# Four doubles of each up projection by Strassen's scheme, in a two-layer decoder trunk

## The chip, the cores and the metric

The kernel runs on one core of one Trainium2 chip. The metric is the device time of one execution in microseconds, median of three runs. Engines are called as the profile calls them: PE is TensorE (PEld its weight loads), DVE VectorE, ACT ScalarE, POOL GpSimd, SP SyncE. A number with an L is a line of the kernel's source.

## The reference

x is one sequence of 512 tokens by 1024 features, all in float32. Layer 0 is a Mamba-2 mixer, then a ConvFFN. Layer 1 is differential attention, then a ConvFFN with weights of its own. The change touches the two ConvFFNs alone:

```python
FFN_DIM = 2816
def conv_ffn(x, ln_g, up_w, conv_w, conv_b, down_w):
    u = causal_dwconv(rms_norm(x, ln_g) @ up_w, conv_w, conv_b)   # width 3 along the tokens
    gate, up = u[..., :FFN_DIM], u[..., FFN_DIM:]
    return (jax.nn.silu(gate) * up) @ down_w
def rms_norm(x, g):
    y = x * lax.rsqrt(jnp.mean(x * x, axis=-1, keepdims=True) + EPS)
    return y * g
...
    x = x + conv_ffn(x, ffn_ln_g[layer], ffn_up_w[layer], ...)
```

## The kernel before

Every product is made three times: an operand is split into a high part (rounded to fp32r by ACT) and a low part (the rest, by DVE), and a product is high x high + high x low + low x high. `mm3` (L207 to L210) issues the three.

The stream x lies transposed in SBUF: features on the partitions, 512 tokens along the free axis, as eight blocks `xT[k]`. For an FFN, `scaled` writes x times the norm's gain into `xgh[k]` and `xgl[k]`. The norm's factor of each token isn't in them; it is a row `rr[0]` (the tile `nr_f`), made from sums over features while the first pair of products runs.

The 2816 features of gate and up are handled as 22 pairs: pair p is 128 columns of gate and the same of up. `products` takes a weight chunk of 1024 x 128 for each and issues 24 matmuls of 512 columns into one PSUM bank. `taps` multiplies the bank by `rr[0]` into `u` (L1021), applies the bias and the last tap on ACT (L1022) and two taps on DVE (L1024). Then follow Silu of gate (L1272), the multiplication (L1276) and `operands`.

The down projection is already done by Strassen's scheme: two pairs (an even and an odd p) by two halves of tokens give a 2 x 2 matrix of operands, and seven products in the order `SEVEN[l]`, named 1 to 7, take the place of eight. `operands` forms the seven operand sides `sh`, `sl` from an even and an odd pair: some are the halves themselves, the others sums of them. Products 5 and 1 in Layer 0, and product 1 in Layer 1, read sides made of the even pair alone. Weights are summed in memory too: `combine` starts accumulating DMAs on POOL's queue.

The pairs come in three parts, `PARTS_D`: pairs 0 to 5, 6 to 13, 14 to 21. After a part's pairs comes its down projection, `down_features` in Layer 0 (matmuls of 256 columns, added to x by L1217) or `down_tokens` in Layer 1 (matmuls of 512 columns, added to `xr` by L1150). In Layer 1 x is first transposed into `xr` (`residual`, L1037).

Weights run through one list, `plan`, in the order in which the products use them. `chunk` hands out the next chunk and first emits those up to two further on: a load on SP's queue, a high split on ACT (L148 or L1079), a low split on DVE (L159 or L1080). There are three raw, three high and three low buffers. A scheduler lays out each engine's instructions before the run, by their place in the program and by when their inputs are ready. In the FFNs PE's order comes from it as well. While Layer 0's FFN runs, `key_weights_in` and `key_weights_out` also scale the key weights for Layer 1 and write them back to memory.

Of the kernel before, what the change touches and what calls it, by code (L numbers as in the profile page):

```python
# [31 lines left out]
PARTS_D = (0, 6), (6, 14), (14, 22)  # L32
# [10 lines left out]
def trunk_kernel(ctx: ExitStack, tc, x, ssm_ln_g, ssm_in_w, ssm_conv_w, ssm_conv_b, ssm_dt_bias,  # L43
# [47 lines left out]

    def ffn_plan(l):
        for p0, p1 in PARTS_D:
            for p in range(p0, p1):
                plan.append(("g%d_%d" % (l, p), *w_cols(ffn_up_w[l], 0, KB, p * P, P)))
                plan.append(("u%d_%d" % (l, p), *w_cols(ffn_up_w[l], 0, KB, FFN + p * P, P)))
            nq = (p1 - p0) // 2
            for m in SEVEN[l]:
                for c in range(0, nq, 2) if l else range(2):
                    plan.append(("s%d%s_%d_%d" % (l, m, p0, c), (l, m, p0, c, min(2, nq - c) if l else nq)))  # L100
# [24 lines left out]
    state = {"next": 0, "use": 0}  # L125
# [3 lines left out]
    class Weights:  # L129


        def __init__(self, i, behind=None):
# [7 lines left out]
            sync.dma_start(self.cols(self.raw), src)  # L140
# [48 lines left out]
    def emit_chunk():  # L189
        i = state["next"]  # L190
        if i < len(plan):
            state["next"] = i + 1
            if len(plan[i]) == 2:
                state["combine"](plan[i][0], *plan[i][1][1:])
                return
            with tc.issue_after(state["rs"]) if i < 5 else nullcontext():
                Weights(i).split()
# [329 lines left out]
    def run(gen):  # L527
        for _ in gen:
            pass
# [435 lines left out]
    def key_weights_in(pl, n, behind):  # L965
        t = pl.tile([P, 1024], F32, tag="stage", name="stage%d" % n, bufs=1)
# [14 lines left out]
    def bias_ranges(pl, behind):  # L981
        rb = pl.tile([AH, 32], F32, name="rb")
# [4 lines left out]
        for i in range(2):  # L987
            bv = pl.tile([AH, hb], F32, name="bv%d" % i)
# [9 lines left out]
    def ffn(l, norm, bp, gnext, nnext):  # L998
        with tc.tile_pool(name="ffn_h%d" % l, bufs=1) as hp, tc.tile_pool(name="ffn%d" % l, bufs=1) as fp:
            rr = []  # L1000

            def products(j, p, c=None):
                key = "%s%d_%d" % ("gu"[j], l, p)
                wh, wl = chunk(key)
                ps = mm_bank("ps_" + key)
                for k in range(KB):
                    last = mm3(ps, wh[:, k, :], wl[:, k, :], xgh[k], xgl[k], k == 0, k == KB - 1)
                    if c is not None and k == KB - 2:
                        with tc.issue_after(last):
                            rr.append(norm.row(c))  # L1010
                return ps

            def taps(j, p, ps):
                key = "%s%d_%d" % ("gu"[j], l, p)
                r = rr[0]
                col = lambda t: cf[l][:, 88 * j + 22 * t + p:88 * j + 22 * t + p + 1]
                u = fp.tile([P, T], F32, tag="u", name="u" + key, bufs=3)
                v = fp.tile([P, T], F32, tag="v%d" % j, name="v" + key, bufs=3 if j else 4)
                if nnext is None and key in ("g1_1", "u1_1"):
                    residual(j)  # L1020
                dve.tensor_tensor(out=u, in0=ps, in1=r, op=ALU.mult)  # L1021
                act.activation(v, u, AF.Identity, bias=col(3), scale=col(2))  # L1022
                for s in range(1, 3):
                    dve.scalar_tensor_tensor(out=v[:, s:], in0=u[:, :T - s], scalar=col(2 - s),  # L1024
                                             in1=v[:, s:], op0=ALU.mult, op1=ALU.add)
                return v

# [26 lines left out]
            def ahead(p0, n, behind):  # L1054

                for k, j, i in (("z", 0, 0), ("x", 0, 1), ("y", 1, 1)) if l else (("x", 0, 0), ("z", 0, 1)):
                    for c in range(0, n // 2, 2) if l else range(2):
                        nq = min(2, n // 2 - c) if l else n // 2
# [677 lines left out]
```

## Time and profile before

| | |
|---|---|
| median of three runs | 1314.41 us (1313.95 to 1314.45) |
| the profiled execution | 1314.37 us, span 1312.7 us |
| busy | PE 1307.3 us, DVE 1073.9, ACT 713.9, POOL 177.1 |
| granted TensorE clock | 1.000 |
| moved by DMA | 167.84 MB, 128 GB/s on average |
| Layer 0's FFN | from 376.6 us to about 728 us of the span |
| Layer 1's FFN | from about 960 us to the end |

A row of a group gives line, engine, operation, names and shapes, count, then busy time and mean duration, then the engine's idle time before these instructions and what ended it. A row in order of time gives start, duration, engine, line, operation. A row by stage gives the stretch, then each engine's busy time and count, the granted clock, and the share and rate of DMA. Matmuls overlap in the trace, so their pace is the distance between starts, not the duration.

### The profile page before, as it was taken

The page shows a single profiled execution, that of the slowest core. Times are in us where ns is not written, and L with a number is a line of the kernel's source. Part 1 is how long each engine was busy: PE and PEld are TensorE (multiplying, and loading weights), DVE is VectorE, ACT ScalarE, POOL GpSimd, SP SyncE. Part 2 cuts the span into 40 slices and gives each one's busy share as a digit, 9 for nine tenths or more (in the row PEclk, how much of TensorE's full clock was granted, in tenths as well). Part 3 has the DMA queues.
Part 4 walks back from the last instruction along what each step waited for, and adds up shares of the span by engine and source line. Part 5 has one row for each costly group of instructions (what it writes and reads, how often), then busy time and mean ns, then how long its engine had stood idle before and what let it go on. Part 6 is the DMA issues. An engine that isn't in the chain of part 4 may idle for free.

```text
span 1312.7 us, 18264 instructions
## 1 busy us (share of the span) xinstructions
PE 1307.3 (100%) x6771; PEld 1096.3 (84%) x6771; DVE 1073.9 (82%) x1774; ACT 713.9 (54%) x1156; POOL 177.1 (13%) x244
## 2 busy tenths in 40 slices
PE   9999999999999999999999999999999999999998
PEld 8878888888888998898889887777888888888887
DVE  7889878888888877876888878678778878887886
ACT  6696554743344545543556667777654544544452
POOL 5330200300021401020113210000020100010001
PEclk9999999999999999999999999999999999999999
DMA  7543533432234656774767763222225446453635
GB/s 210 161 152 87 151 99 108 140 96 82 88 91 137 126 144 200 177 163 121 206 174 150 190 131 114 80 65 69 61 81 160 101 116 191 98 96 113 193 64 128
DMA packets 202552, 167.84 MB, mean 128 GB/s; under 512 B 7580, under 2 KB 175904, under 8 KB 202464
## 3 DMA queue, kind: packets, MB, share of 16 engines
q1 hardware_dynamic: 176080, 124.93, 31.9%
q0 software_dynamic: 22928, 36.46, 14.8%
q10 hardware_dynamic: 3456, 5.30, 1.1%
q8 instruction: 53, 0.87, 0.3%
q14 instruction: 35, 0.29, 0.1%
HBM read 160.21 MB, written 6.44 MB: 127 GB/s over the span
## 4 chain that ended last, share of the span: by engine, by line
PE 99%; ACT 1%; DVE 0%; issue 0%; DVEq 0%
PE ps_g L209 6%; PE ps_u L208 6%; PE ps_g L208 6%; PE ps_u L210 6%; PE ps_g L210 6%; PE ps_u L209 6%; PE ps_in L208 5%; PE ps_in L210 5%; PE ps_in L209 5%; PE ps_s L1239 3%; PE ps_s L1244 3%; PE ps_s L1242 3%; PE ps_s L1146 3%; PE ps_s L1141 3%; PE ps_s L1144 3%; PE ps_o L209 2%
## 5 line engine op out<-in xcount | busy, mean ns | idle before, releaser
L208 PE MATMUL ps_u<-xgh,wh_u 128*128 128x512 f32 x352 | 137.4, 390 | 0.0
L209 PE MATMUL ps_g<-xgl,wh_g 128*128 128x512 f32 x352 | 137.2, 390 | 0.0
L208 PE MATMUL ps_g<-xgh,wh_g 128*128 128x512 f32 x352 | 137.0, 389 | 0.0
L210 PE MATMUL ps_u<-xgh,wl_u 128*128 128x512 f32 x352 | 137.0, 389 | 0.0
L210 PE MATMUL ps_g<-xgh,wl_g 128*128 128x512 f32 x352 | 137.0, 389 | 0.0
L209 PE MATMUL ps_u<-xgl,wh_u 128*128 128x512 f32 x352 | 136.9, 389 | 0.0
L208 PE MATMUL ps_in<-xgh,wh_in 128*128 128x512 f32 x304 | 123.0, 404 | 0.0
L210 PE MATMUL ps_in<-xgh,wl_in 128*128 128x512 f32 x304 | 119.7, 394 | 0.0
L209 PE MATMUL ps_in<-xgl,wh_in 128*128 128x512 f32 x304 | 119.2, 392 | 0.0
L209 PEld LDWEIGHTS ps_g<-xgl,wh_g 128*128 128x128 f32 x352 | 66.1, 188 | 14.3 <-DVE xgl L488 0.7
L210 PEld LDWEIGHTS ps_u<-xgh,wl_u 128*128 128x128 f32 x352 | 66.1, 188 | 13.8
L1244 PE MATMUL ps_s<-sl,wh_s 128*128 128x256 f32 x308 | 77.5, 283 | 0.0
L1242 PE MATMUL ps_s<-sh,wh_s 128*128 128x256 f32 x308 | 77.5, 283 | 0.0
L210 PEld LDWEIGHTS ps_g<-xgh,wl_g 128*128 128x128 f32 x352 | 66.1, 188 | 13.7
L208 PEld LDWEIGHTS ps_g<-xgh,wh_g 128*128 128x128 f32 x352 | 66.0, 188 | 13.6
L208 PEld LDWEIGHTS ps_u<-xgh,wh_u 128*128 128x128 f32 x352 | 66.1, 188 | 13.5
L209 PEld LDWEIGHTS ps_u<-xgl,wh_u 128*128 128x128 f32 x352 | 66.1, 188 | 13.5
L1052 POOL DMA_DIRECT2D wz<-in_ffn_down_w_dram x36 | 44.2, 1294 | 235.2 <-DVE wl_s L1080 167.4
L1126 ACT ACTIVATE sh<-vg 128x256 fp32r<-128x256 f32 (+1 forms) x44 | 23.0, 524 | 97.3 <-DVE vg L1276 97.3
L1272 ACT ACTIVATE vg<-vg 128x512 f32<-128x512 f32 x44 | 27.8, 633 | 78.4 <-DVE vg L1024 78.4
L1024 DVE SCALAR_TENSOR_TENSOR vg<-ug,cf,vg 128x511 f32<-128x511 f32 x88 | 65.8, 748 | 5.5 <-ACT vg L1022 4.1
L1021 DVE TENSOR_TENSOR uu<-ps_u,nr_f 128x512 f32<-128x512 f32 x44 | 30.4, 690 | 48.0 <-PE ps_u L210 48.0
(425 smaller groups left out, 3501.2 us busy)
## 6 DMA issues: line engine op xcount, KB each, us to landing
wr_g<-in_ffn_up_w_dram SPq DMA_DIRECT2D x44, 512.0 KB, 3.9
wr_u<-in_ffn_up_w_dram SPq DMA_DIRECT2D x44, 512.0 KB, 3.9
wr_in<-in_ssm_in_w_dram SPq DMA_DIRECT2D x40, 512.0 KB, 3.9
wz<-in_ffn_down_w_dram POOLq DMA_DIRECT2D x27, 512.0 KB, 5.9
m<-cumd POOLq DMA_DIRECT2D x16, 512.0 KB, 4.3
wr_out<-in_ssm_out_w_dram SPq DMA_DIRECT2D x16, 512.0 KB, 3.4
wr_s<-in_ffn_down_w_dram SPq DMA_DIRECT2D x13, 512.0 KB, 3.7
xT<-in_ffn_down_w_dram SPq DMA_DIRECT2D x10, 512.0 KB, 7.0
```

What stands on the lines that cost most here:

```text
L208: pe.matmul(ps, wh, xh, start=start, stop=False)
L209: pe.matmul(ps, wh, xl, start=False, stop=False)
L210: return pe.matmul(ps, wl, xh, start=False, stop=stop).ins
L1021: dve.tensor_tensor(out=u, in0=ps, in1=r, op=ALU.mult)
L1024: dve.scalar_tensor_tensor(out=v[:, s:], in0=u[:, :T - s], scalar=col(2 - s), in1=v[:, s:], op0=ALU.mult, op1=ALU.add)
L1052: pool.dma_start(view(t, nq), source(p0, c, nq, j, i), accum_op=ALU.add)
L1141: pe.matmul(pss[b], h, ws[q][1][:, cols], start=False, stop=end and q == qs[-1], skip_group_check=more)
L1144: pe.matmul(pss[b], h, ws[q][0][:, cols], start=first and q == qs[0], stop=False, skip_group_check=more)
L1146: pe.matmul(pss[b], w, ws[q][0][:, cols], start=False, stop=False, skip_group_check=more)
L1239: pe.matmul(v[:, b], wl[:, q, cols], h, start=False, stop=q == nq - 1, skip_group_check=not opens or b > 0)
L1242: pe.matmul(v[:, b], wh[:, q, cols], h, start=opens and q + b == 0, stop=False, skip_group_check=not opens or b > 0)
L1244: pe.matmul(v[:, b], wh[:, q, cols], w, start=False, stop=False, skip_group_check=not opens or b > 0)
```

## The change

1. In each layer 8 of the 22 pairs become four doubles: two neighbouring pairs, gate and up, are computed by seven products of 256 features x 512 inputs x 256 tokens (`double`). The 2 x 2 split is over even and odd blocks of inputs, halves of the tokens, and gate against up. The other 14 pairs stay plain; their chunks now hold gate and up of four blocks (`whole`).
2. As a double adds products of different token halves, x must be normalised before it is split. Pairs 0 and 1 still use the old split and the row; meanwhile `normalised`, `split_whole` and `x_sums` make new operands, over `xgh` and `xgl` and in four new tiles. From pair 2 on, the taps read PSUM directly.
3. There are four down parts: pairs 0 to 5, 6 to 11, 12 to 17, 18 to 21. The down projection of a part comes after the first pair of the next part (`D` in `STEPS`); the last one follows its own part.
4. PE runs in program order in the FFNs. `STEPS` is that order: P half a plain pair, a digit one product of a double, D the down projection.
5. `operands` sums in place, without a tile for the sums. In Layer 0 the sides of products 5 and 7 are split together after the odd pair; three operand buffers instead of four.
6. `hooks` start loads when a certain chunk has been emitted. Weights of a double are summed in memory by accumulating DMAs on POOL's queue, and for product 3 by DVE. Staged key weights use the raw buffers.

```diff
-PARTS_D = (0, 6), (6, 14), (14, 22)
+PARTS_D = (0, 6), (6, 12), (12, 18), (18, 22)
+KINDS = "PPP", "PSP", "PSS", "PS"
+STEPS = "PPPPPPPPPPPP", "PPDPP51P26P734PP", "PPD51P26P7345126734", "PPD51P26734P"
...
     def ffn(l, norm, bp, gnext, nnext):
+        with (... tc.manual_schedule(engines={mybir.EngineType.PE})):
...
+            def whole(p, pss):
+                pss += [(aux_bank if j else mm_bank)("ps_%s%d_%d" % ("gu"[j], l, p)) for j in range(2)]
+                for c in range(2):
+                    wh, wl = (t.rearrange("p (k j) c -> p k j c", j=2) for t in chunk("h%d_%d_%d" % (l, p, c)))
+                    for k in range(4):
+                        for j in range(2):
+                            n = 4 * c + k
+                            mm3(pss[j], wh[:, k, j, :], wl[:, k, j, :], xgh[n], xgl[n], n == 0, n == KB - 1)
+                    yield
...
+            def x_sums(k, e, o):
+                e0, e1, o0, o1 = (t[:, :, h * 256:(h + 1) * 256] for t in (e, o) for h in range(2))
+                dve.tensor_tensor(out=e0, in0=e0, in1=e1, op=sub)
+                dve.tensor_tensor(out=e1, in0=o1, in1=e1, op=sub)
+                dve.scalar_tensor_tensor(out=o1, in0=o1, scalar=-1.0, in1=e0, op0=ALU.mult, op1=sub)
+                dve.scalar_tensor_tensor(out=o0, in0=o1, scalar=-1.0, in1=o0, op0=ALU.mult, op1=sub)
+                pieces(*(t[:, k:k + 2] for t in sE), e)
+                pieces(*(t[:, k:k + 2] for t in sO), o)
...
+            def up_combine(key, m, p):
+                if m in "24":
+                    t = wrp.tile([P, 1024], F32, tag="raw", name="wr_" + key)
+                    sync.dma_start(up_view(t), up_source(p, 1, 0 if m == "2" else 1))
...
+                else:
+                    t = ups[p][m in "17"]
+                if m == "3":
+                    dve.tensor_tensor(out=t, in0=t, in1=seconds.pop(p), op=ALU.add)
+                act.activation(wh, t, AF.Copy)
+                dve.tensor_tensor(out=wl, in0=t, in1=wh.bitcast(F32), op=sub)
+                more = {"1": (0, 1), "5": (0, 0)}.get(m)
+                if more:
+                    up_plus(t, p, *more)
...
+            def double(p, sides):
+                ug, uu = u_tile("ug%d_%d" % (l, p)), u_tile("uu%d_%d" % (l, p))
+                for m in "5126734":
+                    wh, wl = chunk("U%d%s_%d" % (l, m, p))
+                    hs, ls = up_side(m)
+                    for b in range(2):
...
+                        for k in range(4):
+                            pe.matmul(ps[b], wh[:, k, cols], hs[:, k, :], ...)
+                            pe.matmul(ps[b], wh[:, k, cols], ls[:, k, :], ...)
+                        for k in range(4):
+                            pe.matmul(ps[b], wl[:, k, cols], hs[:, k, :], ...)
...
+                    elif m == "3":
+                        dve.tensor_tensor(out=ug[:, :, 256:], in0=banks["yt"], in1=ug[:, :, 256:], op=ALU.add)
+                        ga = [taps(0, p + b, ug[:, b]) for b in range(2)]
+                        for b in range(2):
+                            act.activation(ga[b], ga[b], AF.Silu)
+                    elif m == "4":
+                        for b in range(2):
+                            gated(p + b, ga[b], taps(1, p + b, uu[:, b]), sides)
+                    yield
...
             def operands(p, ga, sides):
                 h = ga.rearrange("p (i t) -> p i t", i=2)
                 if p % 2 == 0:
+                    pieces(sh[:, 0], sl[:, 0], h[:, 0])
+                    return
+                sh, sl, e = sides[p - 1]
+                pieces(sh[:, 1:3], sl[:, 1:3], h)
+                e0, e1, o0, o1 = e[:, 0], e[:, 1], h[:, 0], h[:, 1]
...
+                    dve.tensor_tensor(out=e0, in0=e0, in1=e1, op=sub)
+                    dve.tensor_tensor(out=e1, in0=o1, in1=e1, op=sub)
+                    dve.scalar_tensor_tensor(out=o1, in0=o1, scalar=-1.0, in1=e0, op0=ALU.mult, op1=sub)
+                    dve.scalar_tensor_tensor(out=o0, in0=o1, scalar=-1.0, in1=o0, op0=ALU.mult, op1=sub)
+                pieces(sh[:, 3:5], sl[:, 3:5], e)
+                pieces(sh[:, 5:7], sl[:, 5:7], h)
...
             def down_features(p0, n, sides, last):
-                side = {"1": 0, "2": 1, "3": 2, "5": 3, "6": 4, "7": 5, "4": 6}
+                side = {"1": 0, "2": 1, "3": 2, "5": 3, "7": 4, "4": 5, "6": 6}
...
+            quarters = [(0, 0, tmp[0]), (1, 0, tmp[2]), (0, 2, tmp[1]), (1, 2, tmp[3])]
+            u0 = evac(0, ps0)
+            normalised(quarters)
+            for q in quarters[:2]:
+                split_whole(*q)
+            gated(0, *tapped(0, (u0[:, 0], u0[:, 1])), sides)
+            for q in quarters[2:]:
+                split_whole(*q)
+            u1 = evac(1, ps1)
+            for p in range(2, 6):
+                run(plain(p, sides))
...
+                if p == 2:
+                    x_sums(0, tmp[0], tmp[2])
+                elif p == 3:
+                    x_sums(2, tmp[1], tmp[3])
...
+                    if kind == "D":
+                        q0, m = parts[i - 1]
+                        down(q0, m, [behind[q0 + 2 * j] for j in range(m // 2)], False)
+                        gate(sides)
+                        continue
...
+                    next(gens[p])
+                    if kind == "P" and step == 1:
+                        run(gens[p])
+                        if p > p0:
+                            ga = gate(sides)
+                            if p % 2:
+                                stage(ga)
...
+            p0, n = parts[-1]
+            down(p0, n, [sides[p0 + 2 * j] for j in range(n // 2)], True)
```

More of the change, by code (lines that the diff above doesn't have):

```diff
@@ L998, in ffn @@
     def ffn(l, norm, bp, gnext, nnext):
-        with tc.tile_pool(name="ffn_h%d" % l, bufs=1) as hp, tc.tile_pool(name="ffn%d" % l, bufs=1) as fp:
+        with (tc.tile_pool(name="ffn_h%d" % l, bufs=1) as hp, tc.tile_pool(name="ffn%d" % l, bufs=1) as fp,
+              tc.manual_schedule(engines={mybir.EngineType.PE})):
             rr = []
-            def products(j, p, c=None):
-                key = "%s%d_%d" % ("gu"[j], l, p)
[L1004 to L1022, printed above, removed]
@@ new lines, in ffn, with stage, plain @@
+            staged = []
+            count = [0]
+            def stage(u):
+                if l:
+                    return
+                if staged:
+                    key_weights_out(fp, *staged.pop(), u)
+                n = count[0]
+                count[0] += 1
+                staged.append((n, key_weights_in(fp, n, u)))
+            def plain(p, sides):
+                pss = []
+                for _ in whole(p, pss):
+                    yield
+                sides["open"] = p, tapped(p, pss)
```

308 lines of the change are left out of this document (232 added, 76 removed).

## The prediction

> **What bounds the kernel now.** I read the page first, then TensorE's order of time in the first FFN (Layer 0), then the busy times by stage, then VectorE's order of time where the change works.
>
> ```profile
> span 1312.7 us, 18264 instructions
> PE 1307.3 (100%) x6771; PEld 1096.3 (84%) x6771; DVE 1073.9 (82%) x1774; ACT 713.9 (54%) x1156; POOL 177.1 (13%) x244
> PE 99%; ACT 1%; DVE 0%; issue 0%; DVEq 0%
> ```
>
> TensorE (PE) is busy for the whole span and the chain of work runs through nothing else, so only its pace and its waits count. Matmuls overlap in this trace, so the pace is taken from their starts:
>
> ```profile
> 560.48 0.28 PE L1242 MATMUL ps_s<-sh,wh_s 128*128 128x256 f32 x1
> 600.79 0.40 PE L208 MATMUL ps_g<-xgh,wh_g 128*128 128x512 f32 x1
> 687.63 0.39 PE L210 MATMUL ps_u<-xgh,wl_u 128*128 128x512 f32 x1
> 687.86 0.28 PE L1242 MATMUL ps_s<-sh,wh_s 128*128 128x256 f32 x1
> ```
>
> From 560.48 to 600.79 lies the down projection of the second part: 14 chunks of 24 matmuls, 336 in 40.31 us, 0.120 us for one of 256 columns. From 600.79 to 687.86 lie eight pairs of up projection: 384 matmuls in 87.07 us, 0.2267 us for one of 512. Half the columns cost 0.53 of the time. The last up matmul starts 0.23 us before the first down matmul: there is no wait at the change of stage.
>
> ```profile
> core 0: us, PE busy (x) PEld busy (x) DVE busy (x) ACT busy (x) POOL busy (x), PEclk, DMA share, GB/s
> 376.00:443.00 67.00, 67.00 (x300) 54.97 (x299) 55.07 (x88) 31.83 (x44) 15.85 (x33) 1.00 0.46 121
> 376.00:729.00 353.00, 353.00 (x1996) 310.83 (x1995) 284.07 (x398) 179.50 (x234) 60.36 (x90) 1.00 0.62 155
> 960.00:1311.00 351.00, 348.94 (x1561) 288.60 (x1559) 286.57 (x395) 159.90 (x197) 25.74 (x37) 1.00 0.48 123
> ```
>
> The two FFNs keep TensorE full, while VectorE (DVE) stands at 284.07 of 353 us and 286.57 of 351. Its reserve is about 68 us a layer, and the change spends part of it.
>
> **The change, part by part.**
>
> *Doubles.* Two pairs by plain products are 96 matmuls of 512: 21.77 us. A double is 7 products x 2 x 4 x 3 = 168 matmuls of 256: 20.16 us. Saving 1.61 us, eight times: **-12.9 us**. Bounds: 0.1195 and 0.1205 us a matmul (consecutive starts differ by 0.12) give -13.5 to -12.2.
>
> *VectorE's work.* Its pace is read from starts too:
>
> ```profile
> 388.27 0.60 ACT L589 ACTIVATE nr_f<-al_nf 128x512 f32<-128x512 f32 x1 [4.99 <-PE al_nf L524]
> 388.90 0.69 DVE L1021 TENSOR_TENSOR ug<-ps_g,nr_f 128x512 f32<-128x512 f32 x1 [1.77 <-ACT nr_f L589]
> 389.51 0.68 DVE L1021 TENSOR_TENSOR uu<-ps_u,nr_f 128x512 f32<-128x512 f32 x1
> 390.10 1.22 DVE L159 TENSOR_TENSOR wl_g<-wr_g,wh_g 128x1024 fp32r<-128x1024 f32 x1
> 391.24 0.74 DVE L1024 SCALAR_TENSOR_TENSOR vg<-ug,cf,vg 128x511 f32<-128x511 f32 x1
> 391.90 0.74 DVE L1024 SCALAR_TENSOR_TENSOR vu<-uu,cf,vu 128x511 f32<-128x511 f32 x1
> 404.50 0.42 DVE L1124 TENSOR_TENSOR sums<-vg,vg 128x256 f32<-128x256 f32 x1
> 404.84 0.42 DVE L1122 SCALAR_TENSOR_TENSOR sums<-sums,vg 128x256 f32<-128x256 f32 x1
> ```
>
> So 0.60 us for a 512 evacuation, multiply or split, 1.14 for a 1024 split, 0.66 for a tap, 0.34 for a 256 sum. A pair cost 2 evacuations, 4 taps, 1 multiply, 2 weight splits and half of 3.5 us of operand sums: 8.5 us. A plain pair loses the evacuations (7.3); a double takes seven weight splits and one weight add (9.1), four evacuations or sums (1.9), 8 taps (5.3), 2 multiplies and the operands: 21.0 against 17.0. Normalising costs 8 x 0.66, 4 splits and two sets of sums (8 x 0.60, 4 x 1.14): 19.3 us. The fourth down part adds 14 additions of 0.60 in Layer 0 and 18 in Layer 1. A layer: 4 x 4.0 - 12 x 1.2 + 19.3 + 8.4 (10.8) = +29 (+32) us, so 313 to 318 of some 346: 90 to 92%. On average it fits beside TensorE, and its mean costs nothing; what counts is where the work stands in front of a matmul.
>
> *First stretch, pairs 0 to 5.* VectorE gets the norm row at 388.9, 12.3 us after the first up matmul at 376.6:
>
> ```profile
> L208 PE MATMUL ps_g<-xgh,wh_g x352: 388/389/477, 376.6 to 1264.5; 128*128 128x512 f32 x176
> 977.22 1.91 PE L1037 MATMUL xr<-ident,xT 128*128 128x128 f32 x16
> 984.44 1.91 PE L1037 MATMUL xr<-ident,xT 128*128 128x128 f32 x16
> ```
>
> Before the last weight chunk of pair 5 stand, in program order, 4 evacuations 2.4, the scaled copies 5.3, splits of x 4.6, sums of x 9.4, eight weight splits 9.1, taps, multiplies and operands of pairs 0 to 3 20.1: 50.9 us, done 63.2 after the start. TensorE wants the chunk at 60.7 (5 pairs of 10.9, one half, 0.9 of transposes). If the sums of x are put behind the weights the wait is 0; if ScalarE's (ACT) part opens holes between the steps, 5. I take 2 in Layer 0, by the sum, and 1 in Layer 1, where 3.8 us of residual transposes (two rows of 1.91) lengthen TensorE's side. **+3**, bounds 0 to 10. Overwriting x in place follows pair 1 by halves: with two weight splits, an evacuated pair and the scaled copies before it, the first quarter's split ends 22.3 us after the start, and pair 1 ends at 22.8; 0, bounds 0 to 1.
>
> *Third part.* The two adjoining doubles with their pair take TensorE 51.2 us and VectorE 49.3. The end of the first double puts 7.3 us of taps, multiplies and operands (2.6 + 1.2 + 3.5) on VectorE, in program order ahead of the weights of the third product after it, which are due 5.8 us later (two products of 2.9). **+2** for both layers, bounds 0 to 8.
>
> *Last down part.* Here the cover is gone. The order of the last part ends `734P`: the second chunk of pair 19, then at once the down projection, whose first operand pair is 18 and 19. Now the end of a part looks like this:
>
> ```profile
> 688.06 0.69 DVE L1021 TENSOR_TENSOR uu<-ps_u,nr_f 128x512 f32<-128x512 f32 x1 [1.90 <-PE ps_u L210]
> 688.80 0.81 ACT L1022 ACTIVATE vu<-uu,cf 128x512 f32<-128x512 f32 x1
> 690.07 1.53 DVE L1024 SCALAR_TENSOR_TENSOR vu<-uu,cf,vu 128x511 f32<-128x511 f32 x2
> 692.11 0.69 DVE L1276 TENSOR_TENSOR vg<-vg,vu 128x512 f32<-128x512 f32 x1
> 692.83 0.63 ACT L1126 ACTIVATE sh<-vg 128x512 fp32r<-128x512 f32 x1 [1.32 <-DVE vg L1276]
> 697.80 0.95 DVE L1127 TENSOR_TENSOR sl<-sums,sh 128x768 fp32r<-128x768 f32 x1
> ```
>
> From the last up matmul to the last operand pass 11 us (687.63 to 698.75); the first four chunks hide it, because products 5 and 1 of Layer 0 read only the even pair. After the change product 5 reads side 3, which is split together with side 4, and side 4 needs the odd pair. Shortest chain: bias 0.81, four taps 2.6, multiply 0.6, sum 0.34, copy 0.63, five hand-overs of 0.1: 5.5 us. Longest: VectorE first ends the double (2.6 + 1.2 + 3.5 and 1.2 of weights, from 4.2 us before the end), so 4.3 + 2.6 + 0.6 + 0.34 + 0.63 + hand-overs: 9. I take 8, as the double comes first in program order. In Layer 1 product 1 reads the even pair and covers 12 x 0.227 = 2.7 us, product 2 then needs the odd pair's copy: 2 to 5.5, I take 4.5. **+12.5**, bounds 7.5 to 14.5.
>
> *Restart.* The one stretch that follows a long idle TensorE is the start:
>
> ```profile
> 1.14 4.09 PE L292 MATMUL warm<-ones 128*128 128x128 f32 x18 [1.14 <-DVE ones L219]
> 5.06 1.04 PE L309 MATMUL xga<-ident,xt 128*128 128x128 f32 x8
> 6.03 0.23 PE L354 MATMUL ps_dt<-ident,st 8*128 8x8 f32 x1
> ```
>
> 18 matmuls from 1.14 to 5.06 are 0.218 us each, the next eight 0.121: 1.7 us lost. Whether a wait of 4 to 8 us inside the kernel brings it back no row shows: 0 to 1.7 for each of the two, I take 1: **+2**.
>
> [...]
>
> *Queues and the hand-over.*
>
> ```profile
> L1052 POOL DMA_DIRECT2D wz<-in_ffn_down_w_dram x36 | 44.2, 1294 | 235.2 <-DVE wl_s L1080 167.4
> wz<-in_ffn_down_w_dram POOLq DMA_DIRECT2D x27, 512.0 KB, 5.9
> wr_g<-in_ffn_up_w_dram SPq DMA_DIRECT2D x44, 512.0 KB, 3.9
> ```
>
> A double issues four loads on SP (as before) and three accumulating ones on POOL, 1.3 + 5.9 us each; between products 5 and 6 lie three products, 8.6 us, so they are hidden, and POOL has 290 us to spare. In Layer 0 product 5 follows the down part directly, twice: its buffer is freed by product 7 of the down part, five chunks of 2.2 us earlier, against 3.9 + 7.2 + a split: 0 to 2, **+0.5** together. Staged key weights hold one of three raw buffers; a plain chunk lasts 5.4 us against a load of 3.9: 0. ScalarE, at 179.50 of 353 us, gains per layer 20 conversions of 1024 and 28 short copies, under 45 us at 1.1 and 0.7: 0. The last down part of Layer 0 now has 14 chunks of 1.44 us (20.2) against VectorE's 28 x 0.60 and eight splits of x (21.6): **+1**, bounds 0 to 3.
>
> Sum: -12.9 + 3 + 2 + 12.5 + 2 + 0.5 + 1 = +8.1. The profiled execution took 1314.37 us, the median of the runs is 1314.41: **1322 us**.
>
> **The rivals.**
>
> 1. *Faster: the double's operands give way to pair 19.* If VectorE takes pair 19 first, the two waits at the last down parts shrink to 7.5 us together, too short for a slow restart; with the weights in time elsewhere the rest is zero: -5.4, **1309 us**. For it: no FFN wait now, and VectorE's order fills holes with whatever is ready (a weight split stands between evacuation and taps at 390.10). Against it: the double is earlier in program order. It decides once all waits together are under 10.3 us.
> 2. *VectorE becomes the bound.* First stretch 10, third part 8, product 5 4, hand-over 3, last parts 14.5, restarts 3.4: +30, **1344 us** at most, 1332 with half of the first four. For it: 96% of TensorE's time in the third part. Against: TensorE can run on two prepared chunks.
> 3. *Both restarts slow in full*: 3.4 instead of 2, **1324 us**, if the waits outlast what the chip tolerates. [...]
> 4. *Nothing to see:* waits equal the saving, or product matmuls read strided halves more slowly: at 0.1296 us (21.77 / 168) a double saves nothing. The down matmuls at 0.120 have the same shapes, which speaks against the latter. 1312 to 1317 us.
>
> **How the numbers follow.** A change under 0.2% (2.6 us) can't be told from none. My sum 0.30; rival 3 0.18; rival 2 0.14; rival 1 0.25; rival 4 0.13. Slower 0.62, same 0.13, faster 0.25. The likeliest alone spans 1317 to 1328; the range runs from rival 1 with the larger saving (1308) to the middle of rival 2 (1337), leaving out some 0.17 at its ends.
>
> **What would show it.** Right: 1344 matmuls of 256 columns in groups named ps_U at starts 0.120 apart; up matmuls of 512 fallen from 2112 to 1344; a wait of TensorE before product 5 of the last down part in Layer 0 and before product 2 in Layer 1, ended by ScalarE's or VectorE's operand copies; VectorE above 88% in the FFNs. Wrong: no wait of over 3 us there; waits for weights of 5 us and more elsewhere; ps_U at another pace; or a wait for a DMA before product 5.

## The result, and the profile after

| | before | after |
|---|---|---|
| median | 1314.43 us | 1434.95 us |
| ratio | | 1.0918, 95% interval 1.0899 to 1.0937 |
| Layer 0's FFN | 351.6 us | 420.9 us |
| attention | 231.5 us | 239.9 us |
| Layer 1's FFN | 353.0 us | 395.0 us |

The change is 120.5 us slower. The stages here and below run from the first matmul of a stage to the first of the next. From the page of the changed kernel: span and busy time.

```profile
span 1433.2 us, 19941 instructions
PE 1336.2 (93%) x7347; PEld 1138.7 (79%) x7347; DVE 1127.1 (79%) x1871; ACT 771.0 (54%) x1284; POOL 213.5 (15%) x249
```

The busy times by stage (stretch, busy time and count of each engine, granted clock, DMA share and rate):

```profile
377.00:798.00 421.00, 369.00 (x2278) 333.92 (x2277) 303.62 (x434) 202.65 (x290) 82.00 (x96) 0.94 0.62 144
798.00:1038.00 240.00, 233.69 (x1216) 187.01 (x1215) 184.87 (x441) 164.14 (x357) 20.79 (x16) 0.99 0.37 99
1038.00:1433.00 395.00, 358.62 (x1851) 306.15 (x1849) 313.47 (x449) 189.90 (x263) 39.60 (x34) 0.96 0.53 126
```

TensorE was never idle in the FFNs before (the two waits of its whole span, 1.1 and 0.3 us, lie elsewhere); now it is idle for 52 of 421 us in Layer 0, and the clock isn't full any more. TensorE's waits (who waited for whom: us in total, times, longest) name the releasers:

```profile
PE ps_s L1315 <- ACT wh_s L1258: 17.9, 3, 7.0
PE ps_g L243 <- ACT wh_h L182: 12.5, 3, 7.5
PE ps_s L1416 <- ACT sh L1079: 11.2, 3, 10.2
PE ps_U L1171 <- ACT wh_U L1139: 9.1, 3, 4.5
PE ps_U L1171 <- ACT ug L1181: 7.0, 4, 3.8
PE ps_g L245 <- DVE wl_h L193: 6.0, 4, 4.5
PE ps_s L1416 <- ACT wh_s L1258: 4.7, 3, 2.3
PE ps_U L1176 <- DVE wl_U L1140: 4.2, 1, 4.2
PE ps_s L1315 <- ACT sh L1079: 4.1, 3, 2.5
```

All such rows sum to 51.9 us in Layer 0, 6.3 in attention, 29.1 in Layer 1: 87.3. The doubles' matmuls do run at the pace forecast. What is left, 120.5 + 12.9 - 87.3 = 46 us, is two things. One is work at a lower clock: 0.06 x 421 + 0.01 x 240 + 0.04 x 395 = 43 us by the clock column. The other is the end: TensorE's last matmul starts 7.5 us before the end of the span (1425.67 of 1433.2), where it was 4.0 before (1308.66 of 1312.7). VectorE is then still adding the last down part to `xr`, to 1430.0. Matmuls just after two waits, in order of time, beside some at full clock:

```profile
507.14 0.28 PE L1171 MATMUL ps_U<-xgh,wh_U 128*128 128x256 f32 x1
507.26 0.28 PE L1173 MATMUL ps_U<-xgl,wh_U 128*128 128x256 f32 x1
...
516.23 0.79 PE L243 MATMUL ps_g<-xgh,wh_h 128*128 128x512 f32 x1 [7.49 <-ACT wh_h L182]
...
769.66 0.58 PE L1416 MATMUL ps_s<-sh,wh_s 128*128 128x256 f32 x1 [10.23 <-ACT sh L1079]
...
770.85 0.41 PE L1416 MATMUL ps_s<-sh,wh_s 128*128 128x256 f32 x1
771.06 0.41 PE L1418 MATMUL ps_s<-sl,wh_s 128*128 128x256 f32 x1
```

Doubles step by 0.12 us; behind the wait of 10.23 us a matmul of the same 256 columns takes 0.21. The largest releaser, 17.9 us in Layer 1, is a split that itself waited for an accumulating load. The first of its three waits, ScalarE and then TensorE:

```profile
1149.68 1.06 ACT L1258 ACTIVATE wh_s<-wz 128x1024 fp32r<-128x1024 f32 x1 [10.21 <-DMA wz<-in_ffn_down_w_dram]
1150.79 0.79 PE L1315 MATMUL ps_s<-wh_s,sh 128*128 128x512 f32 x1 [5.64 <-ACT wh_s L1258]
```

In Layer 0 the wait of 7.49 us leads back to SP, in order of time:

```profile
489.79 0.37 SPq L172 DMA_DIRECT2D wr_h<-in_ffn_up_w_dram  x1
509.82 0.37 SPq L1004 DMA_DIRECT2D stage<-in_kv_w_dram  x1
510.24 0.46 SPq L172 DMA_DIRECT2D wr_h<-in_ffn_up_w_dram  x1
```

SP issues nothing for 20 us: at its head stands the load of staged key weights, and the plain pair's weights go out 0.42 us after it.

### The profile page after: what moved, and what is told of

Its sections match the earlier page's. It is cut to its first block, busy times and chain, and to the rows that moved or that the text cites. A ratio compares the mean times of both kernels' runs of the same rounds, so it can differ in the third digit from the quotient of the medians.

```text
span 1433.2 us, 19941 instructions
## 1 busy us (share of the span) xinstructions
PE 1336.2 (93%) x7347; PEld 1138.7 (79%) x7347; DVE 1127.1 (79%) x1871; ACT 771.0 (54%) x1284; POOL 213.5 (15%) x249
## 5 line engine op out<-in xcount | busy, mean ns | idle before, releaser
L243 PE MATMUL ps_g<-xgh,wh_h 128*128 128x512 f32 x224 | 89.2, 398 | 12.5 <-ACT wh_h L182 12.5
L193 DVE TENSOR_TENSOR wl_h<-wr_h,wh_h 128x1024 fp32r<-128x1024 f32 x56 | 69.7, 1250 | 35.2 <-ACT wh_h L182 29.0
L182 ACT ACTIVATE wh_h<-wr_h 128x1024 fp32r<-128x1024 f32 x56 | 59.1, 1055 | 71.0 <-PE ps_u L244 32.6
L245 PE MATMUL ps_g<-xgh,wl_h 128*128 128x512 f32 x224 | 89.6, 400 | 6.1 <-DVE wl_h L193 6.0
L243 PE MATMUL ps_u<-xgh,wh_h 128*128 128x512 f32 x224 | 88.8, 396 | 0.0
L244 PE MATMUL ps_g<-xgl,wh_h 128*128 128x512 f32 x224 | 88.5, 395 | 0.0
L244 PE MATMUL ps_u<-xgl,wh_h 128*128 128x512 f32 x224 | 88.5, 395 | 0.0
L245 PE MATMUL ps_u<-xgh,wl_h 128*128 128x512 f32 x224 | 88.3, 394 | 0.0
L1315 PE MATMUL ps_s<-wh_s,sh 128*128 128x512 f32 x153 | 64.6, 422 | 22.0 <-ACT wh_s L1258 17.9
L1416 PEld LDWEIGHTS ps_s<-sh,wh_s 128*128 128x128 f32 x308 | 61.7, 200 | 17.5 <-ACT sh L1079 12.0
```

The lines of the kernel that those rows point to most:

```text
L182: return act.activation(self.wh[:, :self.n], self.raw[:, :self.n], AF.Copy)
L193: return eng.tensor_tensor(out=self.wl[:, :self.n], in0=self.raw[:, :self.n], in1=self.wh[:, :self.n].bitcast(F32), op=ALU.subtract)
L243: pe.matmul(ps, wh, xh, start=start, stop=False)
L244: pe.matmul(ps, wh, xl, start=False, stop=False)
L245: return pe.matmul(ps, wl, xh, start=False, stop=stop).ins
L1315: pe.matmul(pss[b], h, ws[q][0][:, cols], start=first and q == qs[0], stop=False, skip_group_check=more)
```

## The experiments

Medians of all runs, with the ratio to the kernel before and its 95% interval, and the lengths of the three stages in us (e2, e14, e17 and e18 leave the gain out of the keys; e16 is incomplete as said below):

| run | median | ratio | Layer 0 | attention | Layer 1 |
|---|---|---|---|---|---|
| e1 POOL's order | 1413.37 | 1.0752 (1.0736 to 1.0768) | 422.8 | 241.1 | 371.9 |
| e2 no staging | 1393.38 | 1.0604 (1.0588 to 1.0620) | 376.2 | 241.4 | 395.3 |
| e3 kept busy | 1437.00 | 1.0934 (1.0917 to 1.0952) | 424.8 | 240.9 | 393.6 |
| e4 weights first | 1432.46 | 1.0900 (1.0884 to 1.0916) | 419.6 | 241.2 | 393.5 |
| e5 side five | 1433.69 | 1.0912 (1.0885 to 1.0938) | 423.9 | 240.4 | 388.9 |
| e6 half a pair ahead | 1431.83 | 1.0890 (1.0874 to 1.0907) | 422.9 | 241.2 | 390.6 |
| e9 staging early | 1404.44 | 1.0687 (1.0669 to 1.0705) | 391.7 | 239.9 | 393.5 |
| e10 four mends | 1378.71 | 1.0486 (1.0451 to 1.0521) | 385.3 | 241.0 | 372.3 |
| e11 plain pairs | 1386.49 | 1.0545 (1.0527 to 1.0562) | 403.7 | 240.3 | 363.7 |
| e12 fifth mend | 1374.47 | 1.0451 (1.0428 to 1.0475) | 383.4 | 240.8 | 373.8 |
| e13 doubles apart | 1359.03 | 1.0342 (1.0327 to 1.0357) | 376.4 | 241.0 | 365.9 |
| e14 plain, no staging | 1352.18 | 1.0288 (1.0271 to 1.0305) | 368.3 | 241.1 | 364.1 |
| e15 before, raw staging | 1330.05 | 1.0118 (1.0103 to 1.0134) | 366.3 | 231.5 | 353.4 |
| e16 long last part | 1384.42 | 1.0533 (1.0513 to 1.0554) | 408.0 | 232.7 | 367.1 |
| e17 doubles, clean | 1351.44 | 1.0289 (1.0272 to 1.0306) | 363.2 | 241.4 | 366.4 |
| e18 plain, clean | 1345.24 | 1.0231 (1.0216 to 1.0246) | 360.0 | 241.9 | 365.3 |
| e19 long last, doubles | 1367.33 | 1.0399 (1.0381 to 1.0417) | 378.8 | 233.6 | 373.2 |

**e1, POOL's order in Layer 1.**

```diff
-                up_plus(z, p, 1, 1)
+                if summed:
+                    up_plus(z, p, 1, 1)
...
+                if l:
+                    hooks["s16_%d_2" % ...] = lambda p=starts[0]: up_plus(ups[p][0], p, 1, 1, pin)
```

> The changed kernel with one accumulating load moved: in Layer 1 the first sum of a double's weights is issued on POOL's queue behind the down part's last accumulating loads instead of ahead of them. Its plain load stays where it was. Theory (POOL's queue in order): in the changed kernel the down part's product 6 waited 5.64, 7.03 and 5.27 us for an accumulating load that was issued late, because POOL stood at the double's accumulating load, which waited for a plain load to land. These three waits go, and with them the three stretches at half the clock of 6.8 us behind them (about 3 us of slowness each): 1435 - 18 - 9 = about 1408 us. Rival (the transfers are simply too late): the same load is now the last of the queue and the double's first product waits instead; 1430 to 1440 us, with new waits of 3 to 6 us at product 5.

21.6 us less (1434.95 - 1413.37), all of it in Layer 1 (395.0 to 371.9); none of the three waits is left. How POOL delays the first of them shows in the DMA view from 1125 to 1152 us of the changed kernel (name, queue, count, size, median us from issue to landing):

```profile
wz<-in_ffn_down_w_dram POOLq DMA_DIRECT2D x2, 256.0 KB, 9.5
xT<-in_ffn_up_w_dram POOLq DMA_DIRECT2D x1, 512.0 KB, 6.1
```

and from 1128 to 1155 us of e1, which is the same place:

```profile
wz<-in_ffn_down_w_dram POOLq DMA_DIRECT2D x2, 256.0 KB, 6.8
xT<-in_ffn_up_w_dram POOLq DMA_DIRECT2D x1, 512.0 KB, 10.4
```

POOL issued the two kinds within 2 us of each other; the one issued first lands in 6 to 7 us, the other needs 3 to 4 us more. So this wait is more the transfer in front than the late issue that the expectation named.

**e2 and e9, the staging.** e2 makes `stage` return at once and reads the key weights from the input. e9 keeps the staging, but its load no longer waits for a copy on POOL, and its store follows two chunks later:

```diff
-        pool.tensor_copy(t[:, 0:1], behind[:, 0:1])
...
-            act.activation(v[:, k], v[:, k], AF.Copy, scale=g[:, k:k + 1])
+            act.activation(v[:, k], v[:, k], AF.Copy, scale=c2[:, 32 + k0 + k:33 + k0 + k])
...
+                    if staged and staged[0][2] <= state["next"]:
+                        key_weights_out(fp, *staged.pop()[:2], None)
```

> The changed kernel without the staging of the key weights in Layer 0: nothing is loaded, scaled or stored there, and attention reads the key weights from the input, so the gain of their norm is left out of the keys. Theory (the staging holds one of three raw buffers and stands ahead of weight loads and splits on the queues of SP, ACT and POOL): the waits traced to it in Layer 0's FFN, 7.49, 4.49, 3.80, 3.29, 1.68 and some of about 1 us, go, together some 21 us, with about 10 us of restart: about 1404 us, and Layer 1 as in the changed kernel. Rival (VectorE is late there, the staging is only the last of several releasers): under 8 us, 1427 us or more, the waits at the same places ending with VectorE's splits.

> The changed kernel with the staging of the key weights kept whole but let go early: the load waits for nothing on POOL, the scaling reads the gain directly, and the scaling and the store follow two weight chunks after the load, not at the next staging. Theory (what cost 41 us was how long the staging held a raw buffer and stood ahead on the queues, not its work): most of the gain of the kernel without staging comes back, 1395 to 1405 us. Rival (the work itself: 16 scalings on ScalarE and 16 transfers of 512 KB): 1425 us or more, with the waits at the same places.

41.6 us less without staging, 30.5 with the same staging started and let go early. Layer 0 by stage, e2:

```profile
377.00:754.00 377.00, 353.70 (x2280) 323.79 (x2279) 301.13 (x432) 192.46 (x273) 73.14 (x72) 0.97 0.61 138
```

and e9:

```profile
377.00:769.00 392.00, 358.11 (x2278) 327.20 (x2277) 300.48 (x432) 201.21 (x288) 72.79 (x72) 0.96 0.66 154
```

TensorE's idle time falls from 52.0 to 23.3 and 33.9 us, while VectorE does the same 300 to 304 us of work. In the changed kernel a staged block is loaded at 529.08 and stored at 570.02: it holds one of three raw buffers for 41 us, and each weight load that comes to that buffer in turn stands on SP until it is free. The staged loads also stand at the head of SP's queue themselves, until POOL has copied a value of the pair just computed. SP's waits in Layer 0 of the changed kernel, columns as in TensorE's waits:

```profile
SPq L1004 <- POOL gain L1011: 38.7, 6, 18.9
SPq L1004 <- POOL stage L1002: 30.0, 2, 19.7
SPq L172 <- DMA ks<-stage: 20.0, 3, 7.0
```

The first two rows, 68.7 us in eight waits, are the staged loads (15.2 us in the kernel before); the longest one is the 20 us that lead to TensorE's wait of 7.49. In e9 no staged load waits for POOL, and from load to store a block takes 7.4 us on average where it took 34.8. Weight loads that wait for the store of a staged block sum to 36.2 us (the third row and two smaller ones) and still to 34.1 in e9. So the runs show what the staging costs; which of its two delays weighs more isn't separated by a run, though these sums speak for the wait for POOL.

**e4, e5, e3 and e6: one wait at a time.** e4 calls `emit_chunk()` twice ahead of each `x_sums`; e5 makes side 3 in `operands` with the even pair; e3 puts 84 small matmuls ahead of the last down part of Layer 0; e6 has these steps:

```diff
-"PPD51P26P7345126734", "PPD51P26734P"
+"PPDP51P267345126734", "PPDP5126734P"
```

> The changed kernel with two weight chunks emitted ahead of each of the two groups of sums of x in both layers, so that their splits precede the sums in program order. Theory (VectorE does the sums before the next weights' low part): Layer 0's wait of 4.54 us at 427 us and its stretch at half the clock go: 1435 - 4.5 - 2.5 = about 1428 us. Rival: the sums are needed by the first double soon after, which then waits as long: 1433 to 1437 us.

> The changed kernel with the operand side of product 5 made with the even pair again in Layer 0, as the kernel before did, so that products 5 and 1 of the last down part need nothing of the odd pair 19. Theory (the last down part waits for the chain of taps, Silu and operands of pair 19 and 5 reads the end of it): products 5 and 1 are 2 x 24 matmuls at 0.12 us = 5.8 us that run meanwhile; the wait of 10.23 us falls to about 4 and the half clock after it shortens: about 1427 us. Rival (VectorE's backlog, not the order of the sides): the wait falls by under 3 us, as the same VectorE work lies ahead of products 2 and 7: 1432 to 1436 us.

> The changed kernel with 84 small matmuls of ones (0.109 us each, 9.2 us together) ahead of the last down part of Layer 0, which would wait 10.23 us there. Theory (idleness is what halves the clock): no stretch at half the clock from 762 to 776 us, the down part's first matmuls at full pace, some 3 to 4 us less: about 1431 us. Rival (the clock is halved for what TensorE has done before, not for the wait): the same stretches at half the clock, 1434 to 1437 us.

> The changed kernel with another order in parts three and four of both layers: half a plain pair stands between the down part and product 5 of the first double. Theory (product 5 comes too soon after the down part that frees its buffer): the waits of 3.83 and 0.79 us before product 5 in Layer 0 go, with 1.7 us of restart, and the second adjoining double in Layer 1 isn't touched: 1428 to 1431 us. Rival (the accumulating loads on POOL's queue are late by more than half a pair, or the next products now follow each other too closely for VectorE): 1435 us or more, new waits at products 2 and 6.

None gains over 3.2 us, and each interval overlaps that of the changed kernel, so none of these gains is clear of noise; the waits themselves do move. In e4 the wait of 4.54 us is gone, but 2.0 us are waited at 444, and the wait for the staged load at 515 is 7.58 in place of 7.49. In e6 product 5's two waits are gone, and one of 14.1 us before a later product is new, ended by that product's high split. e5, TensorE in order of time behind its last up matmul:

```profile
765.43 0.58 PE L1419 MATMUL ps_s<-sh,wh_s 128*128 128x256 f32 x1 [3.28 <-ACT sh L1079]
771.09 0.50 PE L1416 MATMUL ps_s<-sh,wl_s 128*128 128x256 f32 x2 [0.67 <-DVE wl_s L1259]
774.50 0.51 PE L1416 MATMUL ps_s<-sh,wl_s 128*128 128x256 f32 x2 [1.72 <-DVE wl_s L1259]
779.49 0.58 PE L1419 MATMUL ps_s<-sh,wh_s 128*128 128x256 f32 x1 [3.77 <-ACT wh_s L1258]
784.88 0.39 PE L1419 MATMUL ps_s<-sh,wh_s 128*128 128x256 f32 x1 [2.47 <-ACT wh_s L1258]
```

The wait falls from 10.23 to 3.28, and 8.6 us follow it for weights. For e3, the same place by stage in the changed kernel:

```profile
759.00:770.00 11.00, 0.77 (x3) 0.29 (x2) 9.96 (x20) 5.62 (x10) 2.41 (x2) 0.67 0.23 35
```

and in e3:

```profile
762.00:773.00 11.00, 9.62 (x86) 9.38 (x84) 10.73 (x21) 5.46 (x10) 2.38 (x2) 1.00 0.34 49
```

With TensorE kept busy, 9.62 of 11 us, the clock stays at 1.00 where it was 0.67 with 0.77 us busy: here it was the idle time that lowered it, as the theory said. But the time doesn't fall: from its first matmul the down part takes 29.3 us against 28.6 (773.12 to 802.41; 769.66 to 798.23), as it now waits 4.2 us for a weight where it waited 2.3.

**e10, e12 and e13: mends together.** e10 joins e1, e9, e4 and e5. e12 adds `pin` to the accumulating load of `down_load` in Layer 0. e13 adds the steps:

```diff
-"PPD51P26P7345126734", "PPD51P26734P"
+"PPDP5126734P5126734", "PPDP5126734P"
```

> The changed kernel with four mends together: POOL's order in Layer 1, the early staging, the weights ahead of the sums of x, and product 5's side made with the even pair. Theory (the waits are separate, each with a cause of its own): the gains add up, 21.6 for POOL's order, 30 to 40 for the staging, 2.5 and up to 8 for the other two, which gained little alone because a later wait took it: 1365 to 1375 us. Rival (one engine, VectorE, is simply late, and a mended wait comes back further on): 1385 us or more.

> The kernel with the four mends, and a fifth: in Layer 0 the accumulating loads of the next down part are issued on POOL's queue behind all that stands there in program order, so behind the second double's sums. Theory (POOL's queue in order, as in Layer 1): the wait of 8.94 us in the third part of Layer 0 goes with some 3 us of restart: 1379 - 9 - 3 = about 1367 us. Rival (VectorE's backlog behind the first of two adjoining doubles sets that time, as in Layer 1 where 4.18 us are left): 1374 us or more, the wait shrinking to 4 to 6 us.

> The kernel with five mends and another order in parts three and four: half a plain pair between the down part and the first double, and half a pair between the two doubles that adjoin. Theory (a double needs VectorE and POOL faster than a plain pair, so it must not follow another double or a down part directly): the waits of 3.7 and 1.6 us before product 5 in Layer 0 and of 4.18 us in Layer 1 go: 10 us and some restart less than with five mends, 1352 to 1358 us. Rival (VectorE is late over the whole part, whatever the order): within 4 us of the kernel with five mends, the waits at other products.

The four single gains, 21.6 + 30.5 + 2.5 + 1.3, would give 1379.1; e10 has 1378.71. The two large causes are separate; the two small gains are within noise, and the theory's 8 us for them did not come. e12 gained 4.2, not 12, and its interval overlaps that of e10: the wait in the third part shrank from 8.94 to 6.38 us, so the rival's account, VectorE behind the first of two doubles, fits better. e13 takes them apart and gains 15.4 more. TensorE's longest waits in e12:

```profile
PE ps_U L1173 <- DVE wl_U L1137: 11.4, 3, 6.4
PE ps_U L1168 <- ACT wh_U L1136: 8.2, 4, 3.8
```

and in e13, where the two kinds are down to 2.0 and 1.0 us, the first row is:

```profile
PE ps_U L1168 <- ACT ug L1178: 6.6, 2, 3.4
```

**e11, e14 and e15: which part of the change.** e11 has `KINDS = "PPP", "PPP", "PPP", "PP"`, e14 the same without staging. e15 is the kernel before with one line:

```diff
-        t = pl.tile([P, 1024], F32, tag="stage", name="stage%d" % n, bufs=1)
+        t = wrp.tile([P, 1024], F32, tag="raw", name="stage%d" % n)
```

> The changed kernel with all 22 pairs plain: x normalised in place, the four parts, the down part behind the next part's first pair, the operands made in place and the staging through the raw buffers stay, and so do the sums of x (nothing reads them); the doubles and their summed weights are gone, and the next part's down weights are loaded at the end of a down part. Theory (the doubles' own loads and sums on POOL's queue, and their use of three raw buffers with the staging, bring most of the loss): Layer 1 takes 353 us, 1 for the first stretch, 5 to 6 for the last down part and 3 of restart, about 362; Layer 0 about 352 + 4.5 + 10 + 6 of restart, plus what the staging still costs, 0 to 15; the whole 1340 to 1360 us. Rival (the in-place normalising and the four parts cost as much as the doubles): 1385 us or more, with Layer 1 above 380.

> The changed kernel with plain pairs alone, and without the staging (the gain is left out of the keys). Theory (with plain pairs too, the staging's raw buffer is what delays the weights): the waits of 2.5 to 3.6 us at the first chunk of a pair in Layer 0, five of them, go, with about 2 us of restart each: 1386 - 15 - 3 - 10 = about 1358 us. Rival (the chunks of both gate and up, or the in-place work on VectorE, delay the weights): less than 8 us, 1378 us or more.

> The kernel before with one edit of the change alone: the staged key weights lie in one of the three raw buffers and no longer in a tile of their own. Theory (the staging holds a third of the raw buffers for the time of a pair, and each weight load behind it is late by 2 to 4 us): eight stagings bring waits of 2 to 4 us and 1.7 us of restart each, 30 to 45 us: 1344 to 1360 us. Rival (the prediction's term: a chunk lasts 5.4 us and a load 3.9, so two buffers are enough): within 3 us of the kernel before, 1314 to 1317 us.

Without a double 72.1 of the 120.5 us are still there. (The sums of x are still made in e11, e14, e16 and e18, though nothing reads them there; a plain kernel without them wasn't tried.) Layer 1 is as the theory has it (363.7 for 362), Layer 0 is not. TensorE's first two rows of waits in e11:

```profile
PE ps_g L243 <- ACT wh_h L182: 15.0, 5, 3.6
PE ps_g L245 <- DVE wl_h L193: 7.6, 7, 4.5
```

and in e14:

```profile
PE ps_s L1416 <- ACT sh L1079: 5.4, 1, 5.4
PE ps_g L245 <- DVE wl_h L193: 5.0, 2, 4.5
```

The five waits for a pair's first chunk go with the staging, and 34.3 us with them. In e15 the edit alone costs 15.3 us, between theory and rival: two stagings of eight bring a large wait.

```profile
526.06 0.50 PE L208 MATMUL ps_u<-xgh,wh_u 128*128 128x512 f32 x1 [3.73 <-ACT wh_u L148]
...
660.52 0.65 PE L208 MATMUL ps_u<-xgh,wh_u 128*128 128x512 f32 x1 [3.98 <-ACT wh_u L148]
```

There ScalarE scales the staged block ahead of that split. In the first case it waits 1.56 us, to 522.99, for POOL's copies of the gain, which stand behind two accumulating loads of a down part (519.73 and 521.24 before the wait at 526.06).

**e16 and e19, the hand-over.** e16 is e11 with `PARTS_D = (0, 6), (6, 10), (10, 16), (16, 22)`; in its Layer 1 the third part's down weights are not loaded, so only Layer 0 and the hand-over are read. e19 is e13 with `(0, 6), (6, 12), (12, 16), (16, 22)` and the steps `"PPDP5126734P", "PPD5126734P5126734P"` last.

> The changed kernel with plain pairs alone, and the parts 0 to 5, 6 to 9, 10 to 15 and 16 to 21: the last down part of each layer has three pairs of operands in place of two, the second part two in place of three. Theory (the hand-over to attention is late because 28 additions and the operands of the next stage fall into a last down part of 20 us, now 30): the attention stage falls from 240.3 to about 233 us and Layer 0's last waits shrink: about 1379 us. Rival (the norm and the first splits of attention come behind the last addition whatever its length): the attention stage stays within 2 us of 240: 1384 to 1388 us.

> The kernel with five mends and the doubles apart, staging kept whole, and the parts 0 to 5, 6 to 11, 12 to 15 and 16 to 21: the last down part has three pairs of operands, with two doubles apart in that part. Theory (the hand-over is late because the last down part is short): the attention stage falls from 241 to about 233 us: 1359 - 8 = about 1351 us. Rival (what the hand-over gains, product 5 directly behind the down part gives back): 1356 to 1361 us.

The attention stage of e16:

```profile
785.00:1018.00 233.00, 231.70 (x1215) 186.02 (x1214) 181.93 (x438) 161.84 (x353) 19.03 (x14) 1.00 0.38 103
```

It falls to 232.7 us (233.6 in e19) from 240 to 241, at full clock. So the short last down part is what makes the hand-over late. The end of the span has the same cause: TensorE's last matmul starts 4.2 us before it in e16 and 4.3 in e19, against 8.1 in e13. As a whole e19 is 8 us slower than e13: product 5 directly behind a down part waits 8.1 us in Layer 0, and the last down part of Layer 1, behind a double, 10.0.

**e17 and e18, do the doubles pay when nothing waits on queues?** e17 is e13 without staging, e18 is e14 with the edits of e4 and e5.

> The kernel with five mends and the doubles apart, now without any staging (the gain is left out of the keys). To be set against the next run, which has the same mends, no staging and no doubles. Theory (the doubles' saving arrives once nothing waits on the queues): 10 to 13 us less than the plain one, 1333 to 1340 us. Rival (VectorE's work and the accumulating loads of the doubles cost what their matmuls save): within 4 us of the plain one, about 1345 us.

> Plain pairs alone without staging (the gain is left out of the keys), with the weights ahead of the sums of x and product 5's side made with the even pair. Theory (the two waits at the start and before the last down part of Layer 0 are VectorE's order and cost with their restarts what they show): 4.5 + 2 and 4 + 2 us less than without these two mends, 1340 to 1344 us. Rival (a later wait takes them up, as in the changed kernel): 1348 to 1353 us.

The plain kernel is the faster by 6.2 us, beyond both intervals; the theory had the doubles ahead by 10 to 13. The two FFNs by stage in e17:

```profile
378.00:741.00 363.00, 349.63 (x2277) 320.12 (x2275) 301.01 (x444) 194.08 (x286) 71.47 (x72) 1.00 0.64 144
...
982.00:1348.00 366.00, 350.44 (x1852) 299.62 (x1850) 311.86 (x449) 188.16 (x263) 39.55 (x34) 0.99 0.56 136
```

and in e18:

```profile
377.00:737.00 360.00, 354.74 (x1989) 311.61 (x1988) 278.36 (x410) 172.16 (x244) 55.52 (x60) 1.00 0.54 126
...
979.00:1344.00 365.00, 353.87 (x1562) 290.33 (x1560) 291.98 (x416) 167.02 (x223) 23.98 (x22) 0.99 0.46 119
```

TensorE's busy time falls by 5.1 and 3.4 us, its idle time rises by 8.1 and 4.4 (a few records are missing in Layer 1, in both). VectorE has 23 and 20 us more to do.

## Why the prediction was wrong

That it would be slower came out, by 120.5 us and not by 8. Step by step:

- *Doubles, -12.9.* The pace was right: starts 0.12 us apart (507.14, 507.26), and 2 x 7 x 24 x 4 = 1344 such matmuls. But the saving is only what TensorE could have: between e18 and e17 more idle time takes its place.
- *VectorE's work.* Forecast 313 to 318 us a layer, found 303.6 and 313.5. Rival 2, VectorE as the bound, is not what happened: it is at 72% of a longer stage in Layer 0 and 79% in Layer 1.
- *First stretch, +3.* 4.5 us in Layer 0 and under 1 in Layer 1, of the kind forecast (the sums of x ahead of a low split). Removing it gained 2.5 us (e4), which is within noise.
- *Third part, +2.* 4.2 us in Layer 1 (the row of L1140 above); with the other waits mended, 6.4 more in Layer 0 (e12). The bounds, 0 to 8, hold the first but not the 10.6 of both; taking the doubles apart (e13) took most of them away.
- *Last down part, +12.5.* 10.2 in Layer 0 for 8, and in Layer 1 its six waits sum to 6.0 for 4.5; each a little above its bound.
- *Restart, +2.* **Mis-sized: 43 us.** I counted two long waits; there were 17 stretches at half the clock before the end, 3.4 to 13.7 us long, as waits of 2 to 5 us were everywhere. In the trace half the clock came with each of the ten longest waits in the two FFNs, of 3.80 to 10.23 us. Shorter waits did it too (one of 3.29 us, to 676.01, and below), so rival 1's "too short for a slow restart" doesn't hold.
- *Queues and the hand-over, +1.5.* **This is the step that failed.** Three of its terms, and one that it lacks:
  - "They are hidden", of the accumulating loads: I compared 1.3 + 5.9 us with 8.6 for one load alone and did not ask what else stands on POOL's queue. In Layer 1 the next double's load, put ahead of the running down part's, costs 21.6 us (e1).
  - Staged key weights, "a plain chunk lasts 5.4 us against a load of 3.9: 0": the load's length was compared, but neither what the load itself waits for at the head of SP's queue (68.7 us for POOL) nor how long the buffer is held (34.8 us on average). The staging costs 41.6 us (e2), of which an early start and release bring back 30.5 (e9), and 34.3 in plain pairs (e14); how the two delays share it stays open. I did not follow SP's and ScalarE's queues past the new instructions either: 7.0 us of TensorE's waits are for ScalarE's copies of a bank (row L1181).
  - Hand-over, +1: 8.4 (239.9 - 231.5). I had compared 20.2 us of TensorE with 21.6 of VectorE and taken the difference; e16 and e19 show that the short last part is the cause.
  - The end of the span had no term: 3.5 us more pass behind TensorE's last matmul, and a long last part takes them away too (e19).
- *Product 5, +0.5.* 3.8 and 0.8 us in Layer 0.

So the single waits forecast are where they were said to be; what stands behind the queues, some 63 us by the gains of e1 and e2, was priced at nothing. The sign I named as making the prediction wrong, waits of 5 us and more for weights elsewhere, is what the trace has. The effects are not all independent: e3 to e6 suggest that a mended wait is mostly taken up by the next late thing, while the mends of two queues add up (e10). Left open: of the 30.6 us by which e18 is slower than the kernel before, some 10 are the hand-over, 8 Layer 0's and 12 Layer 1's. Of these 12, 5.1 are TensorE's waits, 3.4 the half clock and 2.3 the later end. A plain kernel with a long last part that computes Layer 1 whole wasn't tried.

No version was faster than the kernel before. The best version of the change that computes everything is e13, 1359.03 us.

## What to carry to other kernels

Before pricing a moved or added DMA at "hidden", list for each queue what stands ahead of it and behind it, what the DMA itself waits for, and for each buffer of a ring how long it is held, not how long its load takes; here one load that waited at the head of SP's queue held up all behind it for 20 us. On a TensorE that never waits, count a saving of matmul time as nothing until every operand still arrives in time: here e17, with the doubles, is 6.2 us slower than e18, without them, and in the changed kernel the waits cost half as much again by the clock (43 us beside 87.3). Mend queues first: here mending one late operand mostly showed the next.

## What the hardware showed

- Waits under 3 us lowered the clock in one place and not in another. In e11 TensorE waited 2.77 and 0.53 us around 542 us, and the clock was at half from 543.8 for 3.4 us; in e17 it stayed at 1.00 over a wait of 2.70 us. Two stretches of e11, then the two of e17 over which its wait is spread:

```profile
540.39:543.80 3.41, 0.73 (x2) 0.30 (x2) 2.92 (x5) 1.81 (x3) 0.00 (x0) 1.00 0.36 135
543.80:547.22 3.42, 3.38 (x8) 2.71 (x9) 1.34 (x2) 0.40 (x1) 0.00 (x0) 0.50 0.86 242
...
621.60:625.01 3.41, 1.83 (x16) 1.63 (x14) 3.32 (x7) 2.32 (x6) 0.00 (x0) 1.00 0.84 132
625.01:628.42 3.41, 2.29 (x19) 2.29 (x20) 3.41 (x6) 1.01 (x2) 0.00 (x0) 1.00 0.02 5
```

TensorE is idle for 2.68 us of the first stretch (3.41 - 0.73), and in the next the clock is 0.50; in e17 it is idle for 1.58 and 1.12 us, and the clock is 1.00 in both. No run varied the length or the place of such a wait alone, so what parts the two cases was not shown.
- At half the clock a matmul of 256 columns stepped by 0.21 us in place of 0.12 (770.85 to 771.06 and 507.14 to 507.26 in the changed kernel). e15 gives a price: 10.0 us of waits, two of them of some 4 us, lengthened the stage by 14.7 us.
